# Measured durations and delays in the table of a kernel's list scheduler

## The chip, the cores and the metric

The kernel runs on one core of a Trainium2 chip. The metric is the time of one execution on the device, in microseconds (us); lower is better. Five engines have a part: TensorE (PE in the profile; PEld is its weight load), VectorE (DVE), ScalarE (ACT), GpSimd (POOL) and SyncE (SP), which issues the DMAs.

## The reference

Two layers of a decoder over 512 tokens of 1024 features, all in fp32. Each layer adds to x, in this order, a mixer, a cross attention into 256 memory tokens (4 heads of 256) and a gated MLP (2816 wide), each on an RMS-normed x:

```
h = rmsnorm(x, norm_mix[l])
x = x + even_mixer(h, ...)   # layer 0: short gated convolution, and causal differential attention, 4 heads
x = x + odd_mixer(h, ...)    # layer 1: stick-breaking attention, 16 heads of 64
x = x + mem_attention(rmsnorm(x, norm_xattn[l]), rmsnorm(mem, norm_mem[l]), ...)
x = x + conv_ffn(rmsnorm(x, norm_ffn[l]), ...)
...
rmsnorm(x, g) = x * rsqrt(mean(x * x) + EPS) * g
conv_ffn(h):  u = causal_dwconv(h @ w_up, w_conv);  gate, val = split(u);  (silu(gate) * val) @ w_down
stick-breaking:  a[t, s] = sigmoid(z_ts) * prod over s < j < t of (1 - sigmoid(z_tj)),  z = q @ k.T / 8
```

## The kernel before

**Data and tiles.** x lies transposed, as eight chunks of 128 features by 512 tokens. Every fp32 operand of a matmul is carried as two float32r parts, hi (the cast) and lo (what the cast leaves), and every product of 128 features is three matmuls: hi by hi, hi by lo, lo by hi. The weights come as 264 slots of 128 x 1024 values (raw, 512 KB each). `prep` makes each slot's hi with a ScalarE cast (L388) and its lo with a VectorE subtraction of raw and hi (L403). Slots belong to groups in the order of the program: V, QK0, A0 and so on for the first mixer, EO0 and EO1 its output, then for layer l KV0_l to KV3_l (keys and values of the memory), Q0_l, Q1_l and XO0_l, XO1_l (the cross attention), U0_l to U10_l and D.._l (the MLP up and down), between them SQK, SV and SO for the stick-breaking heads. A slot of Q0_1, say, is two of eight feature chunks by four column blocks, so one accumulator in PSUM (acc, three of them) takes six matmuls from each of four slots.

**Norms.** `norm_x` starts as soon as a chunk of x has its last sum. For each chunk ScalarE makes the part hs of gain times x (L391), VectorE the other part of it (hs<-x,pp,hs, L409), ScalarE the square (sq), and the squares are summed over the chunks in nacc, by GpSimd (L403 on POOL) and for the last chunk by VectorE. Four matmuls with ones (tr<-ones,nacc) then sum over the features, and the factor is applied after the linear layer, so the first matmuls of that layer need hs and not the factor.

**Heads.** For a head and a block of 128 queries, TensorE makes scores (sc), with kl<-h matmuls of 64 rows for the low part. In the stick-breaking heads ScalarE takes two sigmoids (g), VectorE a scan (L1300) and a product (g<-g,g), POOL cuts a triangle (L457); TensorE then transposes g (tr<-ident,g, L443) and VectorE copies it to pt; after all four blocks the matmuls with the values follow (pv). In the first mixer's differential heads, c and L851 stand at the scan's place, y is a head's output and EO0 takes it.

**What sets the order.** The program is written as some hundred streams (generators) of operations, each with a modelled duration. `Issue.run` keeps a clock for each engine. It takes the engine whose first operation could start earliest, and on it, of those that could start within 0.2 us of that one (0 on PE and SP), the most urgent by the stream's priority. `ready` says when an operation may start: the modelled end of what it reads and overwrites, plus LAT of the engine that produced it. The result is one fixed order on each engine; the hardware then waits on semaphores in that order, and no engine overtakes. So the modelled numbers appear nowhere in the program but in its order.

The stages, in us of the profile: to 60 V and QK0; 60 to 210 the first mixer; 210 to 296 its output, KV0_0 and the norm of the first cross attention; 296 to 396 that attention; 396 to 420 the norm before U0_0; 420 to 756 the first MLP; 756 to 800 the next norm; 800 to 1020 the stick-breaking heads; 1020 to 1105 KV_1, SO1 and the norm before Q0_1; 1105 to 1197 the second cross attention; 1197 to 1220 the norm before U0_1; 1220 to the end the second MLP.

Of the kernel before, what the change touches and what calls it, by code (L numbers as in the profile page):

```python
# [31 lines left out]
def weight_groups():  # L32
    """(name, source, layer, k-chunks, column starts of the 128-wide column chunks)"""
# [176 lines left out]
class Issue:  # L210
# [12 lines left out]
    def ready(self, op):  # L223
        t = 0.0
        for x in op.reads:
            for p in x.parts():
                w, e = x.t.w[p]
                t = max(t, w if e == op.eng else w + LAT.get(e, 0.0))
        for x in op.writes:
            for p in x.parts():  # L230
                w, e = x.t.w[p]
                t = max(t, w if e == op.eng else w + LAT.get(e, 0.0), x.t.r[p])
        return t

    def issue(self, op, start):
# [8 lines left out]
        if op.eng == "SP":  # L244
            self.free_at["SP"] = start + 0.5
            b = max(start + 1.2, self.dma_at)
# [94 lines left out]
def trunk(ctx: ExitStack, tc: tile.TileContext, xT: bass.AP, memT: bass.AP, wts: bass.AP, par: bass.AP, outT: bass.AP):  # L341
# [34 lines left out]
    def act(out, in_, func=AF.Copy, scale=1.0, bias=None, accum=None):  # L376
# [3 lines left out]
        d += 0.093 * (isinstance(scale, V) + (bias is not None) + (accum is not None))  # L380
# [16 lines left out]
    def tt(out, in0, in1, op, eng="DVE"):  # L397
        out, in0, in1 = vw(out), vw(in0), vw(in1)
        d = 0.068 + out.n() / 960.0 if eng == "DVE" else 0.1 + out.n() * 0.0022
        if op == ALU.pow:  # L400
            d = 0.3 + 0.165 * out.n()
# [39 lines left out]
    def tp(out, in_):  # L441
        out, in_ = vw(out), vw(in_)
        return Op("PE", 0.109, [in_, ident_v], [out], lambda: nc.tensor.transpose(out.ap, in_.ap, ident_v.ap))  # L443
# [24 lines left out]
    def stack_q(qs, ps):  # L468
        """qs[s]: rows of part s: hi; the other 64 rows: lo (s = 0, 1: rows 0-63, 64-127 of ps)"""
# [1055 lines left out]
```

## Time and profile before

| | |
|---|---|
| Median of 3 runs | 1575.38 us (1574.05 to 1576.89) |
| Profiled execution, first to last instruction | 1574.8 us (no time of its own stands beside the span) |
| TensorE busy | 1550.8 us, 7242 instructions |
| VectorE, ScalarE, GpSimd busy | 1048.2, 750.0, 175.7 us |
| Mean granted TensorE clock | 0.997 |
| DMA | 146.26 MB, mean 93 GB/s |

Busy time is that of the recorded instructions; matmuls are pipelined, so a busy TensorE has an instruction in it and need not be at its peak. Idle time in brackets names the engine whose result came last. A group joins all instructions of one line and form.

### The profile page before, as it was taken

What the parts mean: (1) busy time and instruction counts of PE and PEld (TensorE: products, weight loads), DVE (VectorE), ACT (ScalarE), POOL (GpSimd) and SP (SyncE); (2) the same over time, 40 slices, a digit from 0 to 9 for tenths busy, and PEclk for the clock granted to TensorE, in tenths of its full rate; (3) what the DMA queues carried; (4) which work ended last, traced back from release to release, by engine and by line L of the source; (5) the groups of instructions that cost most, each with busy time, mean ns of one, the idle gap of its engine ahead of it and who ended that gap; (6) DMA issues with size and microseconds to landing.
All of it is one profiled execution on the core that took longest, in us unless ns stands there. A gap on an engine that the chain in (4) does not pass through costs nothing.

```text
span 1574.8 us, 19182 instructions
## 1 busy us (share of the span) xinstructions
PE 1550.8 (98%) x7242; PEld 1264.2 (80%) x7242; DVE 1048.2 (67%) x1594; ACT 750.0 (48%) x1298; POOL 175.7 (11%) x218
## 2 busy tenths in 40 slices
PE   8999999999999999999999999999999999999999
PEld 6776788788788888888888778787887888888887
DVE  6687756565777457555688887876566765477443
ACT  6566445553534234323577777664544443244221
POOL 4211220200200000000321121202002000000000
PEclk9999999999999999999999999999999999999999
DMA  6212436321233332233221112252113223332232
GB/s 205 70 54 67 127 104 194 110 68 54 64 97 107 107 96 83 89 107 107 81 81 54 48 61 81 80 175 94 54 54 106 88 76 106 107 107 93 76 99 80
DMA packets 42428, 146.26 MB, mean 93 GB/s; under 512 B 4832, under 2 KB 4832, under 8 KB 42336
## 3 DMA queue, kind: packets, MB, share of 16 engines
q1 hardware_dynamic: 42336, 145.04, 29.5%
q8 instruction: 57, 0.93, 0.2%
q14 instruction: 35, 0.29, 0.1%
HBM read 142.92 MB, written 2.10 MB: 92 GB/s over the span
## 4 chain that ended last, share of the span: by engine, by line
PE 88%; DVE 6%; POOL 2%; issue 2%; ACT 2%; DMA 0%; SPq 0%; POOLq 0%; DVEq 0%; ACTq 0%
PE acc L439 77%; PE sc L439 5%; PE pv L439 3%; PE tr L443 3%; POOL nacc L403 2%; DVE hs L409 1%; DVE lo L403 1%; DVE x L403 1%; DMA x<-xT 0%; PE tr L439 0%; ACT hs L391 0%; DVE g L1300 0%; DVE g L403 0%; ACT hi L388 0%; DVE h L403 0%
## 5 line engine op out<-in xcount | busy, mean ns | idle before, releaser
L439 PE MATMUL acc<-hs,hi 128*128 128x512 f32 x1952 | 615.4, 394 | 0.2
L439 PEld LDWEIGHTS acc<-hs,hi 128*128 128x128 f32 x1952 | 365.6, 189 | 78.9 <-issue 3.2
L388 ACT CAST hi<-raw 128x1024 fp32r<-128x1024 f32 (+1 forms) x264 | 271.9, 1035 | 244.4 <-PE acc L439 171.7
L439 PE MATMUL acc<-hs,lo 128*128 128x512 f32 x976 | 383.4, 393 | 4.4 <-DVE lo L403 4.3
L403 DVE TENSOR_TENSOR lo<-raw,hi 128x1024 fp32r<-128x1024 f32 (+1 forms) x264 | 321.9, 1231 | 60.9 <-ACT hi L388 57.9
L439 PE MATMUL acc<-hi,hs 128*128 128x512 f32 (+1 forms) x960 | 280.8, 370 | 0.9 <-ACT hs L391 0.7
L439 PEld LDWEIGHTS acc<-hs,lo 128*128 128x128 f32 x976 | 184.0, 189 | 44.2 <-DVE lo L403 5.7
L439 PE MATMUL acc<-h,hi 128*128 128x512 f32 x704 | 216.2, 389 | 0.0
L439 PEld LDWEIGHTS acc<-hi,hs 128*128 128x128 f32 x960 | 173.1, 190 | 33.6 <-issue 3.1
L439 PE MATMUL acc<-lo,hs 128*128 128x512 f32 (+1 forms) x480 | 176.0, 368 | 5.6 <-DVE lo L403 5.6
L409 DVE SCALAR_TENSOR_TENSOR g<-c,pp,g 128x511 f32<-128x511 f32 (+1 forms) x176 | 132.1, 750 | 56.7 <-ACT g L391 53.6
L403 DVE TENSOR_TENSOR x<-x,acc 128x512 f32<-128x512 f32 x104 | 70.8, 683 | 145.0 <-PE acc L439 144.9
L439 PEld LDWEIGHTS acc<-h,hi 128*128 128x128 f32 x704 | 132.1, 188 | 27.5
L391 ACT ACTIVATE g<-c,pp 128x512 f32<-128x512 f32 x88 | 63.7, 723 | 154.4 <-DVE c L403 154.4
L439 PE MATMUL acc<-h,lo 128*128 128x512 f32 x352 | 136.4, 389 | 0.0
L403 POOL TENSOR_TENSOR nacc<-nacc,sq 128x512 f32<-128x512 f32 x36 | 56.8, 1578 | 524.5 <-ACT sq L391 475.0
L403 DVE TENSOR_TENSOR c<-acc,rrow 128x512 f32<-128x512 f32 x92 | 63.5, 691 | 70.8 <-PE acc L439 63.9
L439 PEld LDWEIGHTS acc<-lo,hs 128*128 128x128 f32 x480 | 90.8, 189 | 22.0 <-DVE lo L403 7.3
L439 PE MATMUL acc<-y,hi 128*128 128x512 f32 x256 | 81.5, 394 | 0.6 <-ACT y L388 0.6
L439 PEld LDWEIGHTS acc<-h,lo 128*128 128x128 f32 x352 | 66.1, 188 | 13.7
L403 DVE TENSOR_TENSOR g<-g,g 128x512 f32<-128x512 f32 (+2 forms) x112 | 64.7, 578 | 7.8 <-ACT g L388 1.4
L391 ACT ACTIVATE g<-sc,rq 128x128 f32<-128x128 f32 (+3 forms) x128 | 60.9, 530 | 8.8 <-PE sc L439 6.5
(157 smaller groups left out, 1624.7 us busy)
## 6 DMA issues: line engine op xcount, KB each, us to landing
raw<-wts SPq DMA_DIRECT2D x256, 512.0 KB, 4.1
x<-xT SPq DMA_DIRECT2D x16, 256.0 KB, 4.8
raw<-wts SPq DMA_DIRECT2D x8, 256.0 KB, 5.9
raw<-memT SPq DMA_DIRECT2D x4, 512.0 KB, 4.2
outT<-x SPq DMA_DIRECT2D x8, 256.0 KB, 2.0
pp<-par SPq DMA_DIRECT2D x1, 303.5 KB, 5.4
pp<-par SPq DMA_DIRECT2D x1, 4.0 KB, 1.7
```

Source lines behind the costliest of these rows:

```text
L388: return nc.scalar.copy(out=out.ap, in_=in_.ap)
L391: return nc.scalar.activation(out=out.ap, in_=in_.ap, func=func, scale=_raw(scale), **kw)
L403: lambda: _ve(eng).tensor_tensor(out=out.ap, in0=in0.ap, in1=in1.ap, op=op))
L409: lambda: nc.vector.scalar_tensor_tensor(out=out.ap, in0=in0.ap, scalar=_raw(scalar), in1=in1.ap, op0=op0, op1=op1))
L439: lambda: nc.tensor.matmul(out.ap, lhsT.ap, rhs.ap, start=start, stop=stop))
L443: return Op("PE", 0.109, [in_, ident_v], [out], lambda: nc.tensor.transpose(out.ap, in_.ap, ident_v.ap))
```

## The change

The table of numbers behind `Issue` is replaced: how long each operation takes, and how long after its end another engine (LAT), and now the same engine (OWN), can use it. No operation is added or removed, and no priority, pool or stream is altered. (Comments and docstrings go too, which moves the line numbers of the new kernel: L403 is L405, L409 is L411, L439 is L443, L1300 is L1304.)

```diff
-LAT = {"PE": 0.25, "ACT": 0.16, "DVE": 0.20, "POOL": 0.10, "SP": 0.0}
+LAT = {"PE": 0.20, "ACT": 0.145, "DVE": 0.12, "POOL": 0.10, "SP": 0.0}
+OWN = {"PE": 0.0, "ACT": 0.135, "DVE": 0.12, "POOL": 0.08, "SP": 0.0}
...
-                t = max(t, w if e == op.eng else w + LAT.get(e, 0.0))
+                t = max(t, w + (OWN if e == op.eng else LAT).get(e, 0.0))
...
-        d = 0.213 if tiny else rhs.n() / 2400.0 + 0.0027
+        d = 0.224 if tiny else max(0.109, (rhs.n() + 32) / 2400.0)
+        if lhsT.ap.shape[0] == 64:
+            d += 0.45
```

The other numbers: a DMA starts 1.7 us after its issue (1.2 before); a ScalarE operation with an accumulator has 0.2 more (0.093); GpSimd's addition is 0.05 + 0.003 n (0.1 + 0.0022 n; for 512 columns 1.59 after 1.23), its power 0.36 + 0.165 n (0.3), its memset 0.1 + 0.0008 n (0.05 + 0.0007 n), its triangle 0.45 + 0.0004 n (0.1 + 0.001 n); VectorE's scan is 0.08 + 0.0021 n (0.068 + n / 960; for 512 columns 1.155 after 0.60); a transpose 0.111 (0.109).

Where the order moves, at three places. In a name such as hs_725_3659 the first number is the tile; a row has line, operation, output and inputs, and its shape.

**The norm before U0_0.** On TensorE, the rows behind the first six matmuls of U0_0, before; acc_736 and acc_739 are the first two accumulators, hi_712 and lo_713 slot U0_0.0, hi_742 and lo_743 slot U0_0.1, hi_749 U0_0.2:

```order
L439 MATMUL acc_736_3705<-hs_725_3659,hi_742_3722 128x512
L439 MATMUL acc_736_3705<-hs_726_3660,hi_742_3722 128x512
L439 MATMUL acc_739_3717<-hs_721_3655,hi_712_3584 128x512
L439 MATMUL acc_739_3717<-hs_722_3656,hi_712_3584 128x512
L439 MATMUL acc_739_3717<-hs_721_3655,lo_713_3585 128x512
L439 MATMUL acc_736_3705<-hs_725_3659,lo_743_3723 128x512
L439 MATMUL acc_736_3705<-hs_727_3661,hi_742_3722 128x512
L439 MATMUL acc_736_3705<-hs_728_3662,hi_742_3722 128x512
L439 MATMUL acc_736_3705<-hs_727_3661,lo_743_3723 128x512
L439 MATMUL acc_736_3705<-hs_729_3663,hi_749_3752 128x512
L439 MATMUL acc_736_3705<-hs_730_3664,hi_749_3752 128x512
L439 MATMUL acc_739_3717<-hs_723_3657,hi_712_3584 128x512
```

Three matmuls of acc_739 stand there twice, each time ahead of a matmul of the first accumulator that reads a low half. The same place on TensorE after (hi_740 is slot U0_0.1, hi_745 U0_0.2):

```order
L443 MATMUL acc_736_3704<-hs_725_3658,hi_740_3720 128x512
L443 MATMUL acc_736_3704<-hs_726_3659,hi_740_3720 128x512
L443 MATMUL acc_736_3704<-hs_725_3658,lo_741_3721 128x512
L443 MATMUL acc_736_3704<-hs_727_3660,hi_740_3720 128x512
L443 MATMUL acc_736_3704<-hs_728_3661,hi_740_3720 128x512
L443 MATMUL acc_736_3704<-hs_727_3660,lo_741_3721 128x512
L443 MATMUL acc_736_3704<-hs_729_3662,hi_745_3734 128x512
L443 MATMUL acc_736_3704<-hs_730_3663,hi_745_3734 128x512
L443 MATMUL acc_736_3704<-hs_729_3662,lo_746_3735 128x512
```

The second accumulator's matmuls (acc_739) no longer stand between those of the first; the first runs straight through its four slots (23 matmuls of the group then stand ahead of tr<-ones,nacc, 22 before). The norm before U0_1 has the same change.

On VectorE from the sum of the sixth chunk of x on, before:

```order
L403 TENSOR_TENSOR x_364_1858<-x_364_1858,acc_718_3626 128x512
L403 TENSOR_TENSOR x_365_1862<-x_365_1862,acc_719_3640 128x512
L409 SCALAR_TENSOR_TENSOR hs_738_3707<-x_364_1858,pp_118,hs_737_3706 128x512
L409 SCALAR_TENSOR_TENSOR hs_741_3719<-x_365_1862,pp_118,hs_740_3718 128x512
L403 TENSOR_TENSOR x_367_1869<-x_367_1869,acc_720_3654 128x512
L403 TENSOR_TENSOR lo_743_3723<-raw_711_3576,hi_742_3722 128x1024
L409 SCALAR_TENSOR_TENSOR hs_748_3747<-x_367_1869,pp_118,hs_747_3746 128x512
L403 TENSOR_TENSOR lo_750_3753<-raw_714_3588,hi_749_3752 128x1024
L403 TENSOR_TENSOR nacc_731_3672<-nacc_731_3672,sq_752_3765 128x512
L403 TENSOR_TENSOR lo_754_3773<-raw_717_3613,hi_753_3772 128x1024
```

All three sums and two of the three hs stand ahead of the first low half. VectorE at the same place after:

```order
L405 TENSOR_TENSOR x_360_1808<-x_360_1808,acc_718_3625 128x512
L411 SCALAR_TENSOR_TENSOR hs_738_3706<-x_360_1808,pp_118,hs_737_3705 128x512
L405 TENSOR_TENSOR x_362_1816<-x_362_1816,acc_719_3639 128x512
L405 TENSOR_TENSOR lo_741_3721<-raw_711_3575,hi_740_3720 128x1024
L411 SCALAR_TENSOR_TENSOR hs_744_3727<-x_362_1816,pp_118,hs_743_3726 128x512
L405 TENSOR_TENSOR x_363_1822<-x_363_1822,acc_720_3653 128x512
L405 TENSOR_TENSOR lo_746_3735<-raw_714_3587,hi_745_3734 128x1024
L411 SCALAR_TENSOR_TENSOR hs_751_3755<-x_363_1822,pp_118,hs_750_3754 128x512
L405 TENSOR_TENSOR lo_753_3762<-raw_717_3613,hi_752_3761 128x1024
L405 TENSOR_TENSOR nacc_731_3672<-nacc_731_3672,sq_755_3773 128x512
```

The low half of U0_0.1 (lo_743, now lo_741) comes one x and one hs earlier, the last hs later, and nacc is behind the low half of U0_0.3 (lo_754, now lo_753) instead of ahead of it.

**The norm before Q0_1.** On VectorE, from the sum of the sixth chunk on, before (lo_1815, lo_1818 and lo_1827 are the slots Q0_1.1 to Q0_1.3):

```order
L403 TENSOR_TENSOR x_364_1858<-x_364_1858,acc_1788_9341 128x512
L403 TENSOR_TENSOR x_365_1862<-x_365_1862,acc_1789_9355 128x512
L409 SCALAR_TENSOR_TENSOR hs_1812_9426<-x_364_1858,pp_118,hs_1811_9425 128x512
L403 TENSOR_TENSOR lo_1815_9440<-raw_1778_9276,hi_1814_9439 128x1024
L409 SCALAR_TENSOR_TENSOR hs_1821_9460<-x_365_1862,pp_118,hs_1820_9459 128x512
L403 TENSOR_TENSOR x_367_1869<-x_367_1869,acc_1790_9369 128x512
L403 TENSOR_TENSOR lo_1818_9455<-raw_1783_9290,hi_1817_9454 128x1024
L409 SCALAR_TENSOR_TENSOR hs_1825_9476<-x_367_1869,pp_118,hs_1824_9475 128x512
L403 TENSOR_TENSOR lo_1827_9483<-raw_1786_9315,hi_1826_9482 128x1024
L403 TENSOR_TENSOR nacc_1805_9391<-nacc_1805_9391,sq_1829_9494 128x512
```

The hs and the low halves alternate there. VectorE at the same place after (lo_1826 is the last of them):

```order
L405 TENSOR_TENSOR x_360_1808<-x_360_1808,acc_1788_9340 128x512
L411 SCALAR_TENSOR_TENSOR hs_1812_9425<-x_360_1808,pp_118,hs_1811_9424 128x512
L405 TENSOR_TENSOR x_362_1816<-x_362_1816,acc_1789_9354 128x512
L405 TENSOR_TENSOR lo_1815_9440<-raw_1778_9275,hi_1814_9439 128x1024
L405 TENSOR_TENSOR x_363_1822<-x_363_1822,acc_1790_9368 128x512
L405 TENSOR_TENSOR lo_1818_9451<-raw_1783_9289,hi_1817_9450 128x1024
L411 SCALAR_TENSOR_TENSOR hs_1821_9460<-x_362_1816,pp_118,hs_1820_9459 128x512
L411 SCALAR_TENSOR_TENSOR hs_1824_9466<-x_363_1822,pp_118,hs_1823_9465 128x512
L405 TENSOR_TENSOR lo_1826_9475<-raw_1786_9315,hi_1825_9474 128x1024
L405 TENSOR_TENSOR nacc_1805_9391<-nacc_1805_9391,sq_1829_9492 128x512
```

The second slot's low half stays behind two sums and one hs; the third's is now ahead of two hs instead of one. On TensorE 25 matmuls of the group, 27 before, stand ahead of tr<-ones,nacc.

**The end of the stick-breaking heads.** On VectorE, up to the product of the last head's last block (the scan is printed as SCALAR_TENSOR_TENSOR at L1300, now L1304), before:

```order
L409 SCALAR_TENSOR_TENSOR hs_1664_8763<-raw_1608_8509,pp_118,hs_1663_8762 128x256
L409 SCALAR_TENSOR_TENSOR hs_1669_8788<-raw_1608_8509,pp_118,hs_1668_8787 128x256
L403 TENSOR_TENSOR pt_1658_8730<-tr_1659_8735,pt_1657_8729 128x128
L403 TENSOR_TENSOR pt_1658_8730<-tr_1660_8737,pt_1657_8729 128x2x128
L403 TENSOR_TENSOR g_1642_8651<-g_1642_8651,g_1641_8650 128x383
L403 TENSOR_TENSOR x_364_1858<-x_364_1858,acc_1646_8679 128x512
L409 SCALAR_TENSOR_TENSOR hs_1669_8788<-raw_1608_8509,pp_118,hs_1668_8787 128x256
L1300 SCALAR_TENSOR_TENSOR g_1647_8684<-g_1647_8684,g_1176_6334 128x512
L403 TENSOR_TENSOR pt_1658_8730<-tr_1670_8802,pt_1657_8729 128x3x128
L403 TENSOR_TENSOR g_1648_8685<-g_1648_8685,g_1647_8684 128x511
```

Copies to pt for the first two blocks (tr_1659, tr_1660) stand shortly ahead of the last scan. VectorE at the same place after:

```order
L405 TENSOR_TENSOR pt_1657_8712<-tr_1659_8719,pt_1656_8711 128x2x128
L411 SCALAR_TENSOR_TENSOR hs_1662_8744<-raw_1611_8527,pp_118,hs_1661_8743 128x256
L405 TENSOR_TENSOR x_357_1798<-x_357_1798,acc_1639_8632 128x512
L411 SCALAR_TENSOR_TENSOR hs_1668_8774<-raw_1611_8527,pp_118,hs_1667_8773 128x256
L405 TENSOR_TENSOR g_1642_8652<-g_1642_8652,g_1641_8651 128x383
L411 SCALAR_TENSOR_TENSOR hs_1668_8774<-raw_1611_8527,pp_118,hs_1667_8773 128x256
L1304 SCALAR_TENSOR_TENSOR g_1646_8673<-g_1646_8673,g_1175_6333 128x512
L405 TENSOR_TENSOR x_358_1802<-x_358_1802,acc_1645_8668 128x512
L405 TENSOR_TENSOR pt_1657_8712<-tr_1669_8782,pt_1656_8711 128x3x128
L405 TENSOR_TENSOR g_1647_8674<-g_1647_8674,g_1646_8673 128x511
```

Between the first sum into x behind the heads' output and that product stood 46 rows, and now 33: the earlier blocks have moved ahead. On TensorE the last four transposes stand 42 rows ahead of KV0_1's first matmul instead of 27, and the three before them 58 instead of 41.

More of the change, by code (lines that the diff above doesn't have):

```diff
@@ L245, in issue @@
             self.free_at["SP"] = start + 0.5
-            b = max(start + 1.2, self.dma_at)
+            b = max(start + 1.7, self.dma_at)
             self.dma_at = b + op.dur
@@ L379, in act @@
         d = (0.051 if in_.psum() else 0.093) + in_.n() / 1200.0
[L380 removed]
+        d += 0.093 * (isinstance(scale, V) + (bias is not None)) + 0.2 * (accum is not None)
         kw = {}
@@ L398, in tt @@
         out, in0, in1 = vw(out), vw(in0), vw(in1)
-        d = 0.068 + out.n() / 960.0 if eng == "DVE" else 0.1 + out.n() * 0.0022
+        d = 0.068 + out.n() / 960.0 if eng == "DVE" else 0.05 + out.n() * 0.003
         if op == ALU.pow:
-            d = 0.3 + 0.165 * out.n()
+            d = 0.36 + 0.165 * out.n()
         return Op(eng, d, [in0, in1], [out],
@@ L442, in tp @@
         out, in_ = vw(out), vw(in_)
-        return Op("PE", 0.109, [in_, ident_v], [out], lambda: nc.tensor.transpose(out.ap, in_.ap, ident_v.ap))
+        return Op("PE", 0.111, [in_, ident_v], [out], lambda: nc.tensor.transpose(out.ap, in_.ap, ident_v.ap))
     def dma(out, in_, n):
@@ L451, in memset @@
         out = vw(out)
-        return Op("POOL", 0.05 + out.n() * 0.0007, [], [out], lambda: nc.gpsimd.memset(out.ap, val))
+        return Op("POOL", 0.1 + out.n() * 0.0008, [], [out], lambda: nc.gpsimd.memset(out.ap, val))
     def affine(out, in_, **kw):
         out, in_ = vw(out), vw(in_)
-        return Op("POOL", 0.1 + out.n() * 0.001, [in_], [out],
+        return Op("POOL", 0.45 + out.n() * 0.0004, [in_], [out],
                   lambda: nc.gpsimd.affine_select(out=out.ap, in_=in_.ap, **kw))
```

4 lines of the change are left out of this document (2 added, 2 removed).

## The prediction

> **What bounds the kernel now.** I read the page's totals and its forty slices first, then its chain that ended last, then a table of busy times by stage, and last the timeline of each engine at the places where that table shows TensorE idle. From the page:
>
> ```profile
> PE 1550.8 (98%) x7242; PEld 1264.2 (80%) x7242; DVE 1048.2 (67%) x1594; ACT 750.0 (48%) x1298; POOL 175.7 (11%) x218
> PE 88%; DVE 6%; POOL 2%; issue 2%; ACT 2%; DMA 0%; SPq 0%; POOLq 0%; DVEq 0%; ACTq 0%
> ```
>
> TensorE is busy 1550.8 of 1574.8 us and makes 88% of the chain; a change of order alone can gain only what it finds in the other 24.0 us and in slow stretches of the busy time. The busy times by stage (start and end, length, then us and instructions of PE, PEld, DVE, ACT, POOL, then TensorE's granted clock, the DMA share and GB/s) say where those lie:
>
> ```profile
> 0.00:60.00 60.00, 55.08 (x246) 43.88 (x247) 40.26 (x64) 36.49 (x65) 23.70 (x28) 1.00 0.49 157
> 60.00:210.00 150.00, 147.81 (x679) 112.95 (x678) 112.90 (x282) 81.14 (x192) 30.76 (x29) 1.00 0.28 87
> 280.00:296.00 16.00, 15.02 (x64) 12.09 (x63) 9.71 (x14) 8.89 (x16) 7.45 (x5) 0.89 0.39 131
> 396.00:420.00 24.00, 21.48 (x92) 16.84 (x91) 19.03 (x20) 11.81 (x17) 11.45 (x7) 0.93 0.30 88
> 420.00:756.00 336.00, 336.00 (x1484) 278.23 (x1483) 208.25 (x257) 125.30 (x156) 0.00 (x0) 1.00 0.31 97
> 800.00:1000.00 200.00, 198.97 (x1070) 156.91 (x1069) 172.50 (x285) 149.65 (x296) 42.02 (x93) 1.00 0.18 54
> 1000.00:1020.00 20.00, 17.92 (x88) 14.48 (x87) 17.24 (x24) 9.96 (x16) 5.87 (x5) 1.00 0.39 113
> 1075.00:1105.00 30.00, 26.65 (x124) 21.27 (x123) 22.14 (x28) 13.87 (x27) 11.40 (x9) 1.00 0.22 70
> 1197.00:1220.00 23.00, 20.49 (x87) 16.07 (x86) 18.25 (x19) 11.12 (x16) 11.45 (x7) 0.93 0.30 85
> 1220.00:1560.00 340.00, 340.00 (x1501) 281.53 (x1500) 208.21 (x258) 121.22 (x150) 0.00 (x0) 1.00 0.30 94
> 1560.00:1574.80 14.80, 11.08 (x49) 8.82 (x47) 2.07 (x3) 0.00 (x0) 0.00 (x0) 1.00 0.19 71
> ```
>
> Length less PE busy is the idle time: 4.92, 2.19, 0.98, 2.52, 0, 1.03, 2.08, 3.35, 2.51, 0 and 3.72, together 23.3 of the 24.0. The two MLPs (676 us) have none, and 336.00 over 1484 rows is 0.226 us a matmul, so nothing can be gained there. The first 60 us wait for inputs and the last 14.8 us hold the last sums and stores (the new order is almost the old one in both). That leaves 14.7 us. Three stretches at half clock come on top; the same table over stretches of 3.41 us:
>
> ```profile
> 405.16:408.57 3.41, 1.27 (x6) 0.76 (x5) 3.41 (x4) 1.96 (x4) 1.99 (x2) 1.00 0.00 0
> 408.58:411.99 3.41, 3.41 (x9) 2.66 (x9) 3.27 (x4) 1.27 (x2) 0.00 (x0) 0.50 0.71 177
> 1084.42:1087.83 3.41, 1.66 (x8) 1.06 (x7) 3.41 (x2) 1.66 (x3) 2.43 (x2) 1.00 0.14 12
> ```
>
> After a stretch in which PE was busy 1.27 us the next ran at 0.50: nine matmuls in 3.41 us, where nine at 0.226 are 2.03, a loss of 1.4. The clock of 0.89 in 280 to 296 and of 0.93 in 1197 to 1220 is the same thing (one such stretch each), so about 4.2 us in all. After 1.66 us busy (1084.42) it did not happen: that row's successor lies in a stage whose clock is 1.00. Ceiling of any gain: 14.7 + 4.2 = 18.9 us, 1.2%.
>
> **The change, part by part.** It adds and removes no instruction; matmuls, weight slots and changes between 128-row and 64-row matmuls (284) are equal in both orders. Only where the order differs can the time differ. The DMA start of 1.7, the memset and the affine select are only modelled numbers too; the order of the slots on SP's queue is the same 264, so I cost them at nothing: the transfers use 0.18 to 0.49 of the DMA engines in the rows above, and that slack covers them. The new matmul duration, 544/2400 = 0.2267 us for 512 columns, is what the MLP rows give; the old 0.216 let the planner's TensorE run 5% ahead.
>
> One thing neither table has. VectorE's timeline at the first MLP's norm, then POOL's, then TensorE's (start, us, engine, line, operation; in brackets the idle time before it and what ended it):
>
> ```profile
> 402.71 3.38 DVE L409 SCALAR_TENSOR_TENSOR hs<-x,pp,hs 128x512 fp32r<-128x512 f32 x2 [0.20 <-ACT hs L391]
> 406.02 0.68 DVE L403 TENSOR_TENSOR x<-x,acc 128x512 f32<-128x512 f32 x1
> 406.62 1.69 DVE L403 TENSOR_TENSOR lo<-raw,hi 128x1024 fp32r<-128x1024 f32 x1
> 408.23 0.74 DVE L409 SCALAR_TENSOR_TENSOR hs<-x,pp,hs 128x512 fp32r<-128x512 f32 x1
> 408.90 1.21 DVE L403 TENSOR_TENSOR lo<-raw,hi 128x1024 fp32r<-128x1024 f32 x1
> 410.03 0.68 DVE L403 TENSOR_TENSOR nacc<-nacc,sq 128x512 f32<-128x512 f32 x1
> 397.30 9.93 POOL L403 TENSOR_TENSOR nacc<-nacc,sq 128x512 f32<-128x512 f32 x6 [49.09 <-ACT sq L391]
> 405.84 0.39 PE L439 MATMUL acc<-hs,lo 128*128 128x512 f32 x1
> 408.36 0.63 PE L439 MATMUL acc<-hs,lo 128*128 128x512 f32 x1 [2.14 <-DVE lo L403]
> 412.57 0.95 PE L439 MATMUL tr<-ones,nacc 128*128 128x1 f32 x8
> ```
>
> While POOL adds nacc (397.30 to 407.23) an hs of VectorE takes 1.7 us (two in 3.38), afterwards 0.74; x, with one input in PSUM, keeps its 0.68. So a duration measured alone is wrong by about 1.0 us for whatever of VectorE's is put beside POOL. The Trainium skill, "SBUF — State Buffer", section "Who interferes with whom", says why: a VectorE instruction with two SBUF inputs and a GpSimd instruction that reads SBUF exclude each other for a whole instruction. The trace agrees (0.74 against 1.7), and the rule speaks against this change: a table of single durations cannot hold it. By the table alone the two MLP norms below would come out at -0.2 each, by the rule at up to +0.6 each.
>
> *The MLP norms (U0_0, U0_1; idle 2.52 and 2.51).* The PE now takes one accumulator through all four slots instead of filling in with a second one; VectorE gets the second low half one x and one hs sooner and has the last nacc behind three low halves instead of two. VectorE's set up to there (three x, three hs, three lo, one nacc) is the same and it is never idle from 402.71 to 411.84, so it ends no earlier. PE has 23 instead of 22 of the group's matmuls before the ones matmuls: -0.23. But lo, 1.69 beside the end of POOL's work, is now beside the middle of it. The second cross attention's norm shows such a one, with its idle PE:
>
> ```profile
> 1082.56 1.70 DVE L409 SCALAR_TENSOR_TENSOR hs<-x,pp,hs 128x512 fp32r<-128x512 f32 x1 [0.19 <-ACT hs L391]
> 1084.18 2.32 DVE L403 TENSOR_TENSOR lo<-raw,hi 128x1024 fp32r<-128x1024 f32 x1
> 1088.72 1.21 DVE L403 TENSOR_TENSOR lo<-raw,hi 128x1024 fp32r<-128x1024 f32 x1
> 1086.56 0.50 PE L439 MATMUL acc<-lo,hs 128*128 128x512 f32 x1 [1.75 <-DVE lo L403]
> 1089.98 0.50 PE L439 MATMUL acc<-lo,hs 128*128 128x512 f32 x1 [1.32 <-DVE lo L403]
> ```
>
> 2.32 - 1.69 = +0.63, and with the -0.23 about +0.3 to +0.4; I take +0.3 each, +0.6 (ends: -1.4 each if the half-clock stretch goes, +1.5 each if one hs more falls beside POOL).
>
> *The second cross attention's norm (Q0_1; idle 3.35).* Here VectorE's third low half goes ahead of an hs, and PE has 25 instead of 27 matmuls before the ones matmuls: two at 0.226, +0.45. The low half that moved up may cost 2.32 instead of 1.21 (+1.1), the hs that moved back 0.74 instead of 1.77 (-1.0, as 402.71 shows); they cancel. +0.5 (ends -1 and +3, the idle time again). What is late next is nacc, behind the same ten operations.
>
> *The first cross attention (idle 0.98).* Only the ones matmuls stand one matmul later: -0.2.
>
> *The end of stick-breaking (idle 2.08).*
>
> ```profile
> 1007.34 0.52 PE L443 MATMUL tr<-ident,g 128*128 128x128 f32 x3 [1.94 <-DVE g L403]
> 1008.12 1.20 DVE L1300 TENSOR_TENSOR_SCAN g<-g,g 128x512 f32<-128x512 f32 x1
> ```
>
> The scan, modelled at 0.60 and now at 1.155, takes 1.20. With it VectorE has 33 rows instead of 46 between the first x after the heads and the last g, and PE asks for the last transposes 15 matmuls earlier, counted from KV0_1 (3.4 us at 0.226). Thirteen rows of 0.6 to 0.7 (x above) are 8 to 9 us less in front of them, so the wait should shrink; but VectorE is busy 17.24 of 20 there, and what stood before the g must be done after it. I take a third of the idle time, -0.7 (ends -2.1 and +1.0).
>
> *The stick-breaking body (idle 1.03) and the layer-0 mixer (2.19).* Between scores and transposes, heads that open a group of four have fewer matmuls than before and the middle ones more, so that gains and losses stand against each other. In the mixer these waits stand:
>
> ```profile
> 66.07 0.63 PE L443 MATMUL tr<-ident,c 128*128 128x128 f32 x4 [0.81 <-DVE c L403]
> 195.38 0.50 PE L439 MATMUL acc<-y,hi 128*128 128x512 f32 x1 [0.59 <-ACT y L388]
> ```
>
> The last values' matmuls come some 10 us of PE work sooner, so the 0.59 for y should go; the diff heads' transposes come closer to their scores, which can cost as much at one of them. 0 for both (ends -3 and +3 together). The cross-attention heads have a little more between score and transpose: -0.2.
>
> Sum: 0.6 + 0.5 - 0.2 - 0.7 + 0 - 0.2 = 0.0. Against the profiled execution's span of 1574.8 that is 1574.8; it lies 0.6 below the median of the runs, 1575.38 (no time of its own stands beside the span), so 1575.4.
>
> **The rivals.**
> (a) Faster: the better numbers for POOL's add, the scan and the 64-row matmul put VectorE's work where PE needs it, at the stick's end, in both mixers and at the norms. Half of the 14.7 us is 7.3: 1568. For it stands the first row of the waits (us in all, times, longest), low halves that come behind other VectorE work:
>
> ```profile
> PE acc L439 <- DVE lo L403: 9.8, 6, 2.1
> ```
>
> Against it: there VectorE is busy all along, so order only moves the wait.
> (b) Faster by the clock: if PE's work fills the stretches before the three slow ones above some 1.6 us, 4.2 us come back: 1571.2. The rule in the Trainium skill, "TensorE: Matmul & The Clock Gate", Part 1, is half rate after at least one idle window of about 3.4 us. By it no stretch of mixed work would be slowed and nothing could come back; the trace differs (1.27 us of PE work, then 0.50). So the trace's condition stands, and small shifts can trip it or not, in both directions.
> (c) Slower: the planner no longer has 5% of PE in hand and its waits are shorter (VectorE's 0.20 became 0.12), so PE's in-order queue reaches a transpose just when the model says that its g is done. Beside POOL's work (42.02 us in 800 to 1000) VectorE is up to 1.0 us late. Of the 64 units of head and block there, four such are 4 us, past what can be told; six give 1581.5. For it: PE cannot overtake. Against it: 198.97 of 200 busy, with the middle heads moved further apart.
> (d) The numbers change the order but not what ends last: the forecast itself.
>
> **Chances.** (d) 0.42, (a) 0.22, (b) 0.10, (c) 0.26. About 0.2% (3.15 us) is what a measurement here can tell from no change; (a) and (b) lie beyond it below, (c) above: faster 0.32, same 0.42, slower 0.26. The range goes from a little under (a), 1567, to (c), 1582; the forecast's own is 1572.5 to 1578.5.
>
> **What would show it.** Right: PE busy all along in both MLPs; idle 2 to 3 us at each MLP norm, with lo as releaser; a shorter wait than 1.94 for g at the stick's end; no wait for y near 195. Wrong: waits of PE for g or c inside 800 to 1000 or 60 to 210 that add up to over 4 us (c), idle time at the norms halved (a), or fewer than two rows at clock 0.50 (b), or more than four.

## The result: slower, 1603 us after 1576

The changed kernel's median is 1602.99 us (four runs, 1596.18 to 1604.97) against 1575.68 for the kernel before on the same chip: a ratio of 1.0159, 95% interval 1.0132 to 1.0187. The forecast was 1575.4, no change, with 1567 to 1582 as its range. The profiled execution is the shortest of the four, with a time of 1596.18 and a span of 1594.4. Its page, the busy times and the share of the chain left aside:

```profile
span 1594.4 us, 19187 instructions
PE 1556.9 (98%) x7242; PEld 1263.7 (79%) x7242; DVE 1050.1 (66%) x1594; ACT 746.7 (47%) x1298; POOL 176.6 (11%) x218
```

The same 7242 matmul records; TensorE is idle 37.5 us where it was 24.0, and busy 6.1 longer. The busy times by stage, with the columns of the prediction's table, show in which stages the idle time grew (the program is up to 20 us later there, so the stretches do not hold quite the same work):

```profile
60.00:210.00 150.00, 141.15 (x642) 106.77 (x641) 109.78 (x276) 79.85 (x191) 29.64 (x26) 1.00 0.25 78
420.00:756.00 336.00, 335.77 (x1486) 277.87 (x1487) 209.27 (x260) 122.22 (x153) 1.02 (x1) 1.00 0.31 99
800.00:1020.00 220.00, 214.82 (x1143) 167.52 (x1142) 187.40 (x305) 158.44 (x312) 44.41 (x97) 0.99 0.19 61
1240.00:1580.00 340.00, 340.00 (x1502) 281.60 (x1501) 208.35 (x258) 121.17 (x150) 0.00 (x0) 1.00 0.29 93
```

The first mixer's 150 us have 8.85 us of idle TensorE instead of 2.19; the MLPs have none, as before. TensorE's waits (us in all, times, longest):

```profile
PE acc L443 <- DVE lo L405: 11.5, 10, 2.2
PE tr L447 <- DVE c L405: 6.2, 6, 2.1
PE tr L447 <- DVE g L405: 1.9, 1, 1.9
PE tr L447 <- DVE sq L405: 1.5, 6, 0.4
```

The row that grew most is the second, transposes of c, 6.2 us now (low halves grew from 9.8 to 11.5). In the kernel before it was

```profile
PE tr L443 <- DVE c L403: 1.2, 2, 0.8
```

The starts of each weight group's first matmul, read off TensorE's timeline, cut the 19.6 us of span by stage:

| from the first matmul of | to that of | before, us | after, us | difference |
|---|---|---|---|---|
| (start) | QK0 | 33.9 | 34.5 | +0.6 |
| QK0 | EO0 (first mixer) | 156.9 | 165.9 | +9.0 |
| EO0 | Q0_0 | 91.2 | 91.8 | +0.6 |
| Q0_0 | Q1_0 (norm) | 27.0 | 25.7 | -1.2 |
| Q1_0 | U0_0 (cross attention) | 94.2 | 95.7 | +1.5 |
| U0_0 | U1_0 (norm) | 28.1 | 27.1 | -1.0 |
| U1_0 | SV0 | 361.2 | 361.2 | 0.0 |
| SV0 | KV0_1 (stick-breaking) | 223.2 | 229.7 | +6.5 |
| KV0_1 | Q0_1 | 67.3 | 67.7 | +0.4 |
| Q0_1 | Q1_1 (norm) | 28.3 | 28.3 | 0.0 |
| Q1_1 | U0_1 (cross attention) | 94.2 | 95.8 | +1.6 |
| U0_1 | U1_1 (norm) | 28.1 | 29.9 | +1.8 |

So heads make it (9.0 + 6.5 + 1.5 + 1.6 = 18.6 of 19.6), not norms. Of the mixer's 9.0 us TensorE's idle time makes 8.1 (1.7 before, 9.7 after, between these matmuls). Of the 6.5 us of the stick-breaking heads it makes only 2.1 (3.1 to 5.2), and the half-clock stretch at 810.95, shown at the end, about 1.7 more (half of its 3.41 us, an estimate). For the other 2.7 us, and for some 1 us in each cross attention, no wait is shown. Many short waits would fit: a 512-column matmul's record lasts 0.39 us while the next starts 0.227 us later, so a wait of under some 0.16 us (an estimate) does not show as idle time.

The median is another 6.8 us above the profiled run, and that part is clock: the four runs' mean granted clocks are 0.996 (1596.18 us), 0.991, 0.991 and 0.989 (1604.97), against 0.997 in the profile of before. Span times mean clock, an estimate of the span without half-clock stretches, is 1588.0, 1586.9, 1586.9 and 1585.6: nearly the same for all four, and a little lower where the clock is lower. For the kernel before (12 runs, 1567 to 1571) its median is 1569.0. So by this estimate some 18 of the 27 us are there in every run. The rest is half-clock stretches: span less full-clock span is 5 us in the median run of before and 14.4 in that of the changed kernel (6.4 to 17.6), and differs from run to run.

### The profile page after: what moved, and what is told of

Read it like the earlier page. It is cut to its first block, busy times and chain, and to the rows that moved or that the text cites. A ratio compares the mean times of both kernels' runs of the same rounds, so it can differ in the third digit from the quotient of the medians.

```text
span 1594.4 us, 19187 instructions
## 1 busy us (share of the span) xinstructions
PE 1556.9 (98%) x7242; PEld 1263.7 (79%) x7242; DVE 1050.1 (66%) x1594; ACT 746.7 (47%) x1298; POOL 176.6 (11%) x218
## 5 line engine op out<-in xcount | busy, mean ns | idle before, releaser
L443 PE MATMUL acc<-hs,hi 128*128 128x512 f32 x1952 | 612.2, 392 | 0.0
L443 PEld LDWEIGHTS acc<-hs,hi 128*128 128x128 f32 x1952 | 366.6, 188 | 75.5 <-issue 1.5
L443 PE MATMUL acc<-hs,lo 128*128 128x512 f32 x976 | 384.2, 394 | 6.3 <-DVE lo L405 6.2
L405 DVE TENSOR_TENSOR lo<-raw,hi 128x1024 fp32r<-128x1024 f32 (+1 forms) x264 | 320.6, 1233 | 63.5 <-ACT hi L390 60.1
L443 PE MATMUL acc<-hi,hs 128*128 128x512 f32 (+1 forms) x960 | 276.5, 367 | 2.0 <-DVE hs L411 1.4
L443 PEld LDWEIGHTS acc<-hs,lo 128*128 128x128 f32 x976 | 183.8, 188 | 47.5 <-DVE lo L405 9.6
L443 PE MATMUL acc<-h,hi 128*128 128x512 f32 x704 | 216.9, 389 | 0.0
L443 PEld LDWEIGHTS acc<-hi,hs 128*128 128x128 f32 x960 | 172.8, 189 | 34.9 <-issue 3.8
L411 DVE SCALAR_TENSOR_TENSOR g<-c,pp,g 128x511 f32<-128x511 f32 (+1 forms) x176 | 132.1, 751 | 75.1 <-ACT g L393 72.0
L443 PE MATMUL acc<-lo,hs 128*128 128x512 f32 (+1 forms) x480 | 176.2, 367 | 5.4 <-DVE lo L405 5.4
L405 DVE TENSOR_TENSOR x<-x,acc 128x512 f32<-128x512 f32 x104 | 71.1, 684 | 142.2 <-PE acc L443 142.0
L443 PEld LDWEIGHTS acc<-h,hi 128*128 128x128 f32 x704 | 132.1, 188 | 27.4
L443 PE MATMUL acc<-h,lo 128*128 128x512 f32 x352 | 137.0, 389 | 0.0
L405 POOL TENSOR_TENSOR nacc<-nacc,sq 128x512 f32<-128x512 f32 x36 | 57.4, 1594 | 531.7 <-ACT sq L393 482.6
L443 PEld LDWEIGHTS acc<-lo,hs 128*128 128x128 f32 x480 | 90.8, 189 | 21.5 <-DVE lo L405 7.5
L405 DVE TENSOR_TENSOR c<-acc,rrow 128x512 f32<-128x512 f32 x92 | 63.3, 688 | 61.1 <-PE acc L443 53.5
L443 PE MATMUL acc<-y,hi 128*128 128x512 f32 x256 | 80.8, 393 | 0.8 <-ACT y L390 0.8
L443 PEld LDWEIGHTS acc<-h,lo 128*128 128x128 f32 x352 | 66.1, 188 | 13.8
L405 DVE TENSOR_TENSOR g<-g,g 128x512 f32<-128x512 f32 (+2 forms) x112 | 64.5, 576 | 7.7 <-ACT g L390 1.4
```

The costliest lines, as they stand in the source:

```text
L405: lambda: _ve(eng).tensor_tensor(out=out.ap, in0=in0.ap, in1=in1.ap, op=op))
L411: lambda: nc.vector.scalar_tensor_tensor(out=out.ap, in0=in0.ap, scalar=_raw(scalar), in1=in1.ap, op0=op0, op1=op1))
L443: lambda: nc.tensor.matmul(out.ap, lhsT.ap, rhs.ap, start=start, stop=stop))
```

## The experiments

The change has three groups of numbers: the latencies (LAT, OWN), TensorE's prices, and the rest (DMA start, ScalarE's accumulator, GpSimd, the scan). Theory A is that the old table had a margin, a TensorE priced 5% too fast and latencies 0.05 us (TensorE's results) and 0.08 us (VectorE's) too long, which hid delays that no table has. Theory B is that a price in the rest is wrong. Theory C is that any new order is a throw of the dice. All runs in one table; "idle" is TensorE's in the two windows of the profiled run, "full clock" the median of span times mean clock, which varies by up to some 5 us between runs of one kernel. Each ratio is to runs of the kernel before on the same chip, whose medians are 1575.7 to 1577.0 us:

| kernel | median us | ratio to before (95%) | idle 60 to 210 | idle 800 to 1020 | full clock |
|---|---|---|---|---|---|
| before | 1575.4 | | 2.2 | 3.1 | 1569.0 |
| changed | 1603.0 | 1.0159 (1.0132 to 1.0187) | 8.9 | 5.2 | 1586.9 |
| lat_old | 1589.7 | 1.0090 (1.0059 to 1.0121) | 6.3 | 4.7 | 1581.2 |
| pe_old | 1581.7 | 1.0036 (1.0025 to 1.0047) | 3.8 | 4.2 | 1576.9 |
| rest_old | 1607.9 | 1.0219 (1.0171 to 1.0267) | 7.8 | 8.0 | 1594.4 |
| rest_new_only | 1579.2 | 1.0009 (0.9996 to 1.0022) | 5.5 | 3.0 | 1575.9 |
| pe_new_only | 1611.2 | 1.0213 (1.0192 to 1.0235) | 7.2 | 10.0 | 1592.1 |
| mm_old | 1581.2 | 1.0027 (1.0006 to 1.0048) | 6.1 | 1.4 | 1571.9 |
| k64_old | 1590.6 | 1.0082 (1.0056 to 1.0107) | 6.5 | 2.6 | 1582.0 |
| pow_long | 1600.5 | 1.0153 (1.0122 to 1.0185) | 7.1 | 5.1 | 1580.5 |
| dice_old | 1584.6 | 1.0050 (1.0033 to 1.0067) | 3.8 | 3.8 | 1571.9 |
| dice_new | 1599.8 | 1.0148 (1.0116 to 1.0181) | 9.1 | 3.5 | 1585.9 |
| pe_fast | 1561.8 | 0.9909 (0.9891 to 0.9926) | 1.8 | 0.8 | 1558.5 |
| lat_wide | 1565.9 | 0.9936 (0.9917 to 0.9955) | 3.0 | 1.6 | 1561.8 |
| new_wide | 1575.6 | 0.9997 (0.9986 to 1.0008) | 3.2 | 1.4 | 1567.3 |
| new_pe_fast | 1601.6 | 1.0163 (1.0148 to 1.0178) | 2.1 | 14.6 | 1580.3 |
| both_old | 1556.8 | 0.9875 (0.9858 to 0.9891) | 0.0 | 0.0 | 1551.8 |
| both_new | 1583.3 | 1.0046 (1.0029 to 1.0062) | 0.1 | 8.3 | 1570.9 |
| both_scan | 1575.2 | 0.9989 (0.9976 to 1.0002) | 0.0 | 8.8 | 1564.1 |
| both_no_scan | 1563.1 | 0.9922 (0.9896 to 0.9947) | 0.1 | 0.0 | 1558.5 |

### Which group of numbers

**lat_old**: the changed kernel with the old latencies.

```diff
-LAT = {"PE": 0.20, "ACT": 0.145, "DVE": 0.12, "POOL": 0.10, "SP": 0.0}
-OWN = {"PE": 0.0, "ACT": 0.135, "DVE": 0.12, "POOL": 0.08, "SP": 0.0}
+LAT = {"PE": 0.25, "ACT": 0.16, "DVE": 0.20, "POOL": 0.10, "SP": 0.0}
+OWN = {"PE": 0.0, "ACT": 0.0, "DVE": 0.0, "POOL": 0.0, "SP": 0.0}
```

> The changed kernel with the latencies put back (LAT 0.25, 0.16, 0.20, 0.10 and no OWN); the new durations stay. Theory A (lost margin: the old table let the planner's TensorE run 5% ahead and its results arrive 0.05 to 0.08 us late, and that margin hid delays that no table has): part of the margin is back, so 1585 to 1597 us, with the waits of TensorE for c in the first mixer (6.2 us in the changed kernel) down to 3 to 5. Theory B (the waits come from prices that are wrong for POOL beside VectorE): latencies do not matter, 1598 to 1605. Theory C (any new order is a throw of the dice): anything from 1575 to 1610, with waits at other places than in the changed kernel.

1589.7 us, inside A's range: half of the loss comes back (at full clock a third, 1581.2 after 1586.9). But not where A said: the waits for c were to fall to 3 to 5 us, and are 6.5 (6.2 in the changed kernel).

**pe_old**: the changed kernel with TensorE's old prices (the transpose's 0.109 too).

```diff
-        d = 0.224 if tiny else max(0.109, (rhs.n() + 32) / 2400.0)
+        d = 0.213 if tiny else rhs.n() / 2400.0 + 0.0027
-            d += 0.45
+            d += 0.0
```

> The changed kernel with TensorE's old durations (n/2400 + 0.0027, no 0.45 for 64 rows, 0.213, 0.109); latencies and all other durations stay new. Theory A: the 5% is the larger part of the margin, so 1577 to 1588 us and waits for c under 3 us. Theory B: 1598 to 1605. Theory C: 1575 to 1610.

1581.7, inside A's range, and 1.0 us of waits for c (6.2 in the changed kernel).

**rest_old**: the changed kernel with the old prices of the rest.

```diff
-            b = max(start + 1.7, self.dma_at)
+            b = max(start + 1.2, self.dma_at)
...
-        yield Op("DVE", 0.08 + w * 0.0021, [gv, mv], [qv],
+        yield Op("DVE", 0.068 + w / 960.0, [gv, mv], [qv],
```

> The changed kernel with the old durations of DMA start, ScalarE's accumulator, GpSimd's addition, power, memset and triangle, and VectorE's scan; latencies and TensorE's durations stay new. Theory A: the scan and the additions were then planned shorter than they are (0.60 for 1.2, 1.23 for 1.6), so the margin is smaller still: 1603 to 1612. Theory B: these prices are the cause, so 1575 to 1585. Theory C: 1575 to 1610.

1607.9, in A's range. B falls in this form: the old prices of the rest do not bring the time back. **rest_new_only** has the latencies and TensorE's prices old together, **pe_new_only** TensorE's prices new and all else old (the same edits, combined).

> The old latencies and TensorE's old durations, with the other new durations (DMA start, accumulator, GpSimd, scan): the old margin with the better prices. Theory A (lost margin): as fast as the kernel before or a little faster, 1568 to 1578 us, since the runs so far give +8 for these prices old and the margins new. Theory C (any new order is a throw of the dice, and the kernel before a lucky one): 1580 to 1610.

1579.2, a little above A's range and not to be told from the kernel before (0.9996 to 1.0022). The better prices of the rest brought nothing where the old margin stood. By waits they did harm: TensorE is idle 5.5 us in the mixer, after 2.2, and the full-clock span is 6.9 us longer (1575.9). The median hides it because these runs had fewer half-clock stretches (median clock 0.999).

> Only TensorE's durations new; latencies and all others old. Theory A: TensorE's 5% is most of the margin, so 1590 to 1605 us, with waits of TensorE for transposes (c, g, pt) of over 6 us. If the margin needs both parts to go: 1578 to 1585.

1611.2, worse than the whole change and above A's range. So TensorE's measured prices alone cost 34 us; that the other two groups give some back (8 us) is within what a new order alone can do, as the next section shows. Within that price, **mm_old** keeps the 0.45 and puts the matmul back to n/2400 + 0.0027, **k64_old** drops the 0.45 and keeps (n + 32)/2400.

> The changed kernel with the old price of a matmul (n/2400 + 0.0027) but with 0.45 for one with 64 rows. If the matmul's 5% is the margin: 1578 to 1586 us, the mixer's waits gone, as with all of TensorE's durations old (1581.7). If the 0.45 made the loss: 1598 to 1605.

> The changed kernel without the 0.45 for a matmul of 64 rows; all else new. If the matmul's 5% is the margin: 1595 to 1605 us. If the 0.45 made the loss (it moves only the stages with such matmuls, 60 to 210 and 800 to 1020 us): 1578 to 1586.

mm_old has 1581.2, the time expected of the 5%, but not its place: the mixer's waits were to be gone, and TensorE is still idle 6.1 us there (3.6 us of waits for c in all), while the stick-breaking window went from 5.2 to 1.4. k64_old has 1590.6, between the two forecasts: the 0.45 has a part (12 us in the median, 5 at full clock), but with the 5% back it costs nothing in the median (mm_old and pe_old are alike). So the price of a matmul is the larger part, and its waits do not sit in one place.

### How much is the throw of the order

**dice_old** prices a matmul 0.0005 us higher in the kernel before, **dice_new** 0.0004 us higher in the changed one.

```diff
# dice_old
-        d = 0.213 if tiny else rhs.n() / 2400.0 + 0.0027
+        d = 0.213 if tiny else rhs.n() / 2400.0 + 0.0032
# dice_new
-        d = 0.224 if tiny else max(0.109, (rhs.n() + 32) / 2400.0)
+        d = 0.224 if tiny else max(0.109, (rhs.n() + 33) / 2400.0)
```

> The kernel before with the price of a matmul raised by 0.0005 us (0.2165 for 0.2160), all else old: an order that differs in some hundreds of rows, with the same margin. It measures how far the throw of a new order alone moves the time. Theory A: within 4 us of before, 1573 to 1581. Theory C: 1580 to 1605.

> The changed kernel with the price of a matmul raised by 0.0004 us ((n + 33)/2400), all else as changed: the same throw on the other side. Theory A: like the changed kernel, 1596 to 1608. Theory C: anything, below 1590 as likely as above.

dice_new behaves as A said (1599.8). dice_old is 8.7 us slower than before, outside A's range and inside C's. At full clock it is 2.9 us slower (1571.9), the rest is clock (median 0.993). So in these two throws a new order was worth up to 3 us of waits and up to 6 of clock, and differences under 10 us in the table are not to be read one by one. Two throws do not say how far one can go. That the 27 us are not a throw rests on them and on the whole table: without wide latencies, the seven kernels with the measured price of a matmul lie at 1589.7 us and above, and the five with its old price at 1584.6 and below.

### One chain looked at closely

The chain behind the new waits for c: VectorE's sum (s), GpSimd's power (s<-s,mhalf), VectorE's s,k and c, then TensorE's transposes. The timelines of GpSimd, VectorE and TensorE in the changed kernel, at two of its eight norms:

```profile
55.13 2.71 POOL L405 TENSOR_TENSOR s<-s,mhalf 128x8 f32<-128x8 f32 x1 [4.99 <-DVE s L421]
63.15 3.68 POOL L405 TENSOR_TENSOR s<-s,mhalf 128x8 f32<-128x8 f32 x1 [5.32 <-DVE s L421]
62.99 2.35 DVE L405 TENSOR_TENSOR lo<-raw,hi 128x1024 fp32r<-128x1024 f32 x2
58.98 0.63 PE L447 MATMUL tr<-ident,c 128*128 128x128 f32 x4 [1.12 <-DVE c L405]
68.03 0.63 PE L447 MATMUL tr<-ident,c 128*128 128x128 f32 x4 [2.11 <-DVE c L405]
```

The power is priced 1.68 us and takes 1.64 alone. Beside two low halves of VectorE in a row (62.99, 2.35 us) it took 3.68, 2.0 more, and TensorE waited 2.11. In the kernel before the same place had one low half beside it and 2.55 us. Of the changed kernel's 6.2 us of waits for c, though, 2.6 stand behind powers of the ordinary length: at 132.24 us, for one, TensorE waited 1.24 us after a power of 1.64, because VectorE had a low half (130.00, 1.23 us) ahead of s,k. **pow_long** adds 1.0 us to that price alone.

```diff
-            d = 0.36 + 0.165 * out.n()
+            d = 1.36 + 0.165 * out.n()
```

> The changed kernel with 1.0 us more for GpSimd's power alone (1.36 + 0.165 n for 0.36 + 0.165 n), nothing else. In the changed kernel the power of 8 columns takes 2.5 to 3.7 us where VectorE subtracts a low half beside it, 1.64 alone and 1.68 in the table, and TensorE then waits for c at the eight norms of queries and keys in the first mixer. If that chain makes the waits there, TensorE's idle time between 60 and 210 us falls from 8.9 us to 3 to 5 and the time to 1594 to 1599 us. If the mixer's waits have another cause, or move to the next thing, 1600 to 1606 us.

The same two places in its timelines:

```profile
55.05 1.64 POOL L405 TENSOR_TENSOR s<-s,mhalf 128x8 f32<-128x8 f32 x1 [4.32 <-DVE s L421]
63.13 2.55 POOL L405 TENSOR_TENSOR s<-s,mhalf 128x8 f32<-128x8 f32 x1 [6.44 <-DVE s L421]
59.68 0.63 PE L447 MATMUL tr<-ident,c 128*128 128x128 f32 x4 [0.69 <-DVE c L405]
67.28 0.63 PE L447 MATMUL tr<-ident,c 128*128 128x128 f32 x4 [0.48 <-DVE c L405]
```

The waits of 1.12 and 2.11 are 0.69 and 0.48, all waits for c 3.8 instead of 6.2, and the full-clock span is 6 us shorter (1580.5 for 1586.9). But the idle time in the window is 7.1, not the 3 to 5 expected, and the median, 1600.5, is inside the range that stood for another cause (1600 to 1606); these runs had more half-clock stretches (clock 0.984 to 0.992). The chain is at most part of the loss.

### Margin the other way

**pe_fast** is the kernel before with a matmul priced lower still; **lat_wide** the kernel before with longer latencies; **both_old** has both.

```diff
# pe_fast
-        d = 0.213 if tiny else rhs.n() / 2400.0 + 0.0027
+        d = 0.2 if tiny else rhs.n() / 2640.0 + 0.0027
# lat_wide
-LAT = {"PE": 0.25, "ACT": 0.16, "DVE": 0.20, "POOL": 0.10, "SP": 0.0}
+LAT = {"PE": 0.25, "ACT": 0.40, "DVE": 0.45, "POOL": 0.45, "SP": 0.0}
```

> The kernel before with one number changed the other way: a matmul of n columns priced n/2640 + 0.0027 (0.197 us for 512, 13% under the 0.2267 measured; 0.2 for the tiny ones), all else old. Theory A (the margin of TensorE's price hides delays that no table has): no slower than before, 1568 to 1578 us, with idle time in the first mixer at or below the 2.2 us of before. Theory C (any new order is a throw of the dice around 1590, and the kernel before a lucky one): 1580 to 1605.

> The kernel before with longer latencies alone: 0.40, 0.45 and 0.45 us for results of ScalarE, VectorE and GpSimd (0.16, 0.20, 0.10), all else old. Theory A: each chain of five engine changes is planned some 1.2 us longer, so fewer waits for transposes, 1568 to 1578 us. Theory C: 1580 to 1605. If wide latencies cost in another way (accumulators and buffers held longer, work for TensorE missing), 1580 to 1590 with TensorE waiting for nothing that a transpose needs.

1561.8 and 1565.9: both faster than before, by more than A asked for and far below C. A price that is 13% too low made a better order than the measured one.

> The kernel before with both margins: matmul n/2640 + 0.0027 and the wide latencies, all else old. If margins add: 1553 to 1560 us (pe_fast had 12 us of idle and half-clock time left to gain in the first 1550). If pe_fast has taken what there is: 1559 to 1566. If too much margin holds buffers and starves TensorE: above 1568.

1556.8 us (1553.38 to 1557.54), 1.25% faster than the kernel before: the margins add in part (14.0 and 10.0 us apart, 19.7 together), and this is the version that beats both kernels. Its page has

```profile
PE 1542.4 (99%) x7242; PEld 1265.6 (81%) x7242; DVE 1042.7 (67%) x1594; ACT 741.9 (48%) x1298; POOL 176.0 (11%) x218
```

(TensorE busy 8.4 us less than before for the same matmuls), and its two windows of heads are

```profile
60.00:210.00 150.00, 149.97 (x696) 116.56 (x695) 114.21 (x289) 85.53 (x202) 31.28 (x29) 1.00 0.29 91
800.00:1020.00 220.00, 220.00 (x1160) 175.40 (x1160) 189.68 (x306) 157.63 (x310) 45.46 (x95) 1.00 0.23 69
```

TensorE is idle 0.03 us in the first mixer and not at all in the stick-breaking stage (5.3 together in the kernel before). The delay is still there: GpSimd's power at 62.72 us takes 2.54, as the 2.55 of the kernel before, and TensorE waits for c nowhere, after 0.81 us there and 2.11 in the changed kernel. The margin did not make the power faster; TensorE has other matmuls to do until c is there.

**new_wide** is the changed kernel, every measured duration and OWN kept, with lat_wide's latencies; **new_pe_fast** the changed kernel with pe_fast's price and no 0.45.

> The changed kernel with all its measured durations, but latencies of 0.25, 0.40, 0.45 and 0.45 us for results of TensorE, ScalarE, VectorE and GpSimd. If any margin does, wherever in the table it stands: 1565 to 1578 us, waits for c under 2 us. If TensorE's price must be low (an order planned with a fast TensorE is better for another reason, such as more work held ready for it): 1585 to 1600.

> The changed kernel with a matmul priced n/2640 + 0.0027 and no 0.45, the shorter latencies and the other measured durations kept. If the margin does it: 1565 to 1577 us, below the 1581.7 with n/2400. If the short latencies still let through what the price hides: 1578 to 1590.

new_wide has 1575.6: margin in the latencies alone takes back the whole loss with TensorE at its measured price. So it is margin as such that was missing, not a low price. new_pe_fast has 1601.6, which neither expectation had. Its mixer is mended and its stick-breaking stage broken, as the two windows show:

```profile
60.00:210.00 150.00, 147.90 (x679) 113.18 (x678) 114.09 (x283) 83.16 (x196) 31.11 (x29) 1.00 0.27 87
800.00:1020.00 220.00, 205.45 (x1052) 161.90 (x1050) 166.08 (x266) 137.24 (x265) 29.25 (x81) 0.96 0.17 53
```

### Where a low price does harm

**both_new** is both_old with the measured prices of the rest, **both_scan** with the scan's alone, **both_no_scan** with all of them but the scan's.

```diff
# both_scan, against both_old
-        yield Op("DVE", 0.068 + w / 960.0, [gv, mv], [qv],
+        yield Op("DVE", 0.08 + w * 0.0021, [gv, mv], [qv],
```

> Both margins with the other measured durations (DMA start, accumulator, GpSimd, scan). If the measured prices help once the margin is there: 1 to 5 us below the run with both margins and old prices. If they only reshuffle, as with the old margin (1579.2 against 1576.9): within 4 us of it, or above.

> The kernel with both margins and old prices (1556.8 us), with the scan's measured price alone (0.08 + 0.0021 n for 0.068 + n/960: 1.155 for 0.60 us at 512 columns, which the traces confirm). VectorE is busy 190 of the 220 us of the stick-breaking stage and TensorE's work there, priced 13% low, comes to some 191: with the true scan the planner sees VectorE as the bottleneck there. If that is why the measured prices cost 26 us with both margins: 1572 to 1586 us, TensorE busy under 214 of 220 us in 800 to 1020. If another price does it: 1553 to 1562.

> The kernel with both margins and the measured prices of DMA start, accumulator and GpSimd, the scan's price old. If the scan alone makes the 26 us: 1553 to 1563 us, TensorE busy over 217 of 220 us in 800 to 1020. If GpSimd's prices do: 1570 to 1586.

both_new lost 26 us to both_old (1583.3). The scan alone makes 18 of them (both_scan 1575.2). The others make 6 (both_no_scan 1563.1, just past the 1563 expected if the scan alone did it), which is no more than a throw. both_scan's stick-breaking window:

```profile
800.00:1020.00 220.00, 211.19 (x1087) 165.01 (x1087) 181.14 (x288) 147.54 (x287) 36.50 (x90) 0.98 0.20 60
```

8.8 us idle where both_old has none, with a scan price that is the right one (1.155 for the 1.20 of the trace). With TensorE at its old or true price the right scan does no such harm (rest_new_only 3.0 and new_wide 1.4 us idle there). So it is the pair of prices that hurts, not the scan's alone. A reason that fits these runs: VectorE is busy 190 of 220 us there, and with TensorE 13% too fast and VectorE true the planner's VectorE is the fuller engine, so that it orders for the wrong bottleneck. The planner's own clocks were not looked at; this reason is argued, not shown.

## Why the prediction was wrong

**What bounds the kernel.** Right: TensorE, nothing in the MLPs, and a ceiling of some 19 us for a gain. both_old took 19.7 us in the median, a little above the 18.9, and 17.2 at full clock.

**The step that failed** is the term for the stick-breaking body and the layer-0 mixer, "0 for both (ends -3 and +3 together)". The two measured +6.5 and +9.0. The sign that the prediction had set for rival (c), over 4 us of waits for g or c inside these windows, came: 5.8 us between 60 and 210. Its signs for itself failed: the wait for g at the stick's end stayed 1.9 us, and the wait for y is 0.8 us at 204.69 instead of none. The working had seen that diff heads' transposes "come closer to their scores" and let that cancel against the wait for y. It read margins in matmuls from the order, and did not ask whether what was left covered the delays. That it did not is what the runs show: wider latencies alone, with every measured duration kept, took the loss back (new_wide, 1575.6). One of those delays is in the eight norms of queries and keys of the mixer. Each has a power on GpSimd, and VectorE delayed three of them in the changed kernel, by 0.9 to 2.0 us. The prediction looked at VectorE delayed by GpSimd and never at GpSimd delayed by VectorE, though the kernel before has it (2.55 against 1.64 us):

```profile
53.92 1.64 POOL L403 TENSOR_TENSOR s<-s,mhalf 128x8 f32<-128x8 f32 x1 [4.34 <-DVE s L419]
62.38 2.55 POOL L403 TENSOR_TENSOR s<-s,mhalf 128x8 f32<-128x8 f32 x1 [6.82 <-DVE s L419]
```

There TensorE's wait was 0.81 (the row at 66.07 in the prediction), against 2.11 in the changed kernel. Which delays make the +6.5 of the stick-breaking heads stays open: idle time explains 2.1 of it.

**The cross-attention heads**: -0.2 was forecast, +1.5 and +1.6 came (the two rows of the table from Q1 to U0).

**The norms**: +0.6 for the MLP's two, measured -1.0 and +1.8, in sum +0.8; +0.5 for Q0_1, measured 0.0; -0.2 for Q0_0, measured -1.2. All four together were +0.9 and measured -0.4. They decided nothing, and the +1.8 holds a double half-clock stretch (1230.78) where the kernel before has a single one, 1.7 us of it by an estimate; so the two that look right in sum are partly luck. **The end of stick-breaking**: the -0.7 did not come; the wait of TensorE for g there is 1.9 us after as before.

**The rivals.** (c) was the right mechanism, at the wrong place and too small: it named the lost 5% and the shorter latencies, but counted only units of the stick-breaking stage, six at 1.0 us, and ended at 1581.5 (1575.4 and 6.0 are 1581.4). The mixer had more than that stage. (b) was right that small shifts trip the clock, and the time went the other way: half-clock stretches cost the changed kernel 9 us more in the median run. The range, built on (c)'s 1581.5, took neither in.

**GpSimd beside VectorE.** The Trainium skill, "SBUF — State Buffer", section "Who interferes with whom", says that whichever of the two starts first blocks the other. The trace agrees for GpSimd as the one blocked: its power takes 1.64 us alone and 3.68 beside 2.35 us of VectorE's subtractions. The prediction used one direction of that rule.

## What to carry to other kernels

Where an order is fixed ahead and engines cannot overtake, a measured duration is not the best number for the planner: a result that comes late stops the queue, one that comes early only holds a buffer, so plan with margin. Here 0.24 to 0.35 us more on the hand-overs of three engines, with TensorE priced 13% low, gave 1.25%; no larger margin was tried. Where the other prices are measured ones, put the margin in the hand-over times and not in one engine's price: new_wide has 1575.6 us, new_pe_fast 1601.6. With the old prices the low price did as well as the wide hand-overs (1561.8 and 1565.9). When a diff makes a model truer, ask first what its errors were hiding. And test a scheduler's number with a neighbour 0.0005 us away, to know how much of a difference is the throw.

## What the runs showed of the hardware

Half-clock stretches inside a trace are 3.41 us long or a multiple, and their number differs between runs of one program: rest_old ran from 1603.2 us (clock 0.996) to 1619.6 (0.985) with a full-clock span of 1593.4 to 1596.4. A kernel with more waits does not always have more of them: pe_old and rest_new_only have more idle time than the kernel before and a higher median clock (0.998 and 0.999, the kernel before 0.996 to 0.997). Two of the changed kernel's stretches (the second a double one), each with the window ahead of it, from its table of busy times:

```profile
807.53:810.94 3.41, 2.39 (x10) 1.43 (x10) 1.60 (x4) 3.02 (x6) 0.58 (x2) 1.00 0.44 155
810.95:814.36 3.41, 3.41 (x14) 2.61 (x12) 2.07 (x5) 2.16 (x5) 1.10 (x2) 0.53 0.00 0
1227.37:1230.78 3.41, 1.17 (x6) 0.76 (x5) 3.41 (x5) 2.54 (x4) 1.36 (x1) 1.00 0.37 142
1230.78:1237.60 6.82, 6.82 (x22) 5.45 (x21) 2.73 (x4) 0.59 (x1) 1.02 (x1) 0.51 0.73 233
```

A window with 2.39 us of busy TensorE was followed by half clock, though the prediction's one with 1.66 was not. In the first, seven of the ten matmuls have 256 columns or fewer: counted as columns at 0.2267 us for 512 it holds, by an estimate from the timeline, some 1.1 us of work, and the one with 1.66 some 1.4 to 1.5. So busy time of the records is not what decides. Columns alone do not decide either: in lat_wide, half clock came at 144.41 us after a window with 3.41 us busy and, by the same count, some 1.6 us of columns. What does stays open.
